# A layer kernel: the long convolution's result written over its padded input, two more PSUM banks for the last fill products, and a diagonal product in two fp32r parts

## The chip, the cores and the metric

The kernel runs on one core of one Trainium2 chip. The metric is the device time of one execution in microseconds (us), and the time of a kernel is the median of its runs. A core has five engines with an instruction stream each: PE (TensorE, matrix products; its weight loads are shown apart as PEld), DVE (VectorE), ACT (ScalarE), POOL (GpSimd) and SP (SyncE, which here issues the DMAs). Each engine works through its own instructions in a fixed order and waits where the next one needs a result or a buffer that is not there yet. Products are summed in PSUM, which has eight banks of 128 partitions by 512 fp32 numbers.

## The reference, cut to what matters

One layer over 1024 tokens of width 1024. A modulated norm feeds one input projection, and its columns feed three mixers: a neighbourhood attention, a short gated convolution and a Conformer branch with a 31-tap depthwise convolution and a layer norm behind it. The three are merged by gates, and an output projection follows.

```python
def dw_conv(x, w):
    k = w.shape[0]
    return lax.conv_general_dilated(x, w[:, None, :].astype(x.dtype), window_strides=(1,),
        padding=[((k - 1) // 2, k // 2)], dimension_numbers=('NWC', 'WIO', 'NWC'),
        feature_group_count=x.shape[-1])

def conformer_branch(z, w_conv, b_conv, ln_g, ln_b):
    a, g = z[..., C_GLU:C_GLU + D_BRANCH], z[..., C_GLU + D_BRANCH:C_Z]
    u = dw_conv(a * jax.nn.sigmoid(g), w_conv) + b_conv
    u = jax.nn.silu(layer_norm(u, ln_g, ln_b))
    return u * jax.nn.silu(z[..., C_Z:GATES])

def merge_branches(z, ya, yb, yc, w_out_a, w_out_b, w_out_c, w_o):
    ga, gb, gc = jnp.split(jax.nn.sigmoid(z[..., GATES:]), N_BRANCH, axis=-1)
    m = ga * (ya @ w_out_a) + gb * (yb @ w_out_b) + gc * (yc @ w_out_c)
    return m @ w_o

# hybrid_layer
h, gate = modulate(x, c, lp['norm_g'], lp['w_ada'], lp['b_ada'])
z = h @ lp['w_in']
x = x + gate * merge_branches(z, ya, yb, yc, lp['w_out_a'], lp['w_out_b'], lp['w_out_c'], lp['w_o'])
```

## The kernel before

**Numbers in two parts.** Nearly every product of two fp32 matrices is done as three products of type fp32r: both factors are split into a rounded part (`wh`, `bh`: an ACT copy) and the rest (`wl`, `bl`: a subtraction on DVE or POOL), and wh·bh, wh·bl and wl·bh are summed in one bank. `split` does this. So each weight tile costs ACT a copy and DVE or POOL a subtraction before PE can use it. One product of 128 rows by 512 columns over a depth of 512 is 12 matmuls in a row.

**The stages.** Up to about 490 us the norm, the q, k and v projections and the attention run. Beside the attention PE is kept filled with "fill" products: `first_quarters` computes, for 20 of the 22 pairs of column tiles that come later, the product of one quarter (24 matmuls in two parts of 12, `quarter_part`) into a bank `qps` and sends each part's result to memory (`p1d` after part 0, `c11d` or `gd` after part 1). The last `BEHIND` = 4 fill products stand after the attention (L817). From 513 us on `group` (L885 to L945) is run 22 times, with seven multiplications of halves in place of eight, some of them already done by the fill: PE computes the products `gf`, `gc`, `gd`, `ge`, DVE adds them up (`u2` L919, `v` L923, and `c22`, `c12`, `c21` in `add`, L876), and a second product is summed into the bank of `gd` once `c22` has been read from it. PE's order puts the products `ge`, `gf` and `gc` between the end of `gd` and that second product (`gd<-hb`). Behind the groups come the merges of the three branches (`merge(1)`, `merge(0)`, `merge(2)`, with the products `ops` of L108 to L110) and the output projection, to the end.

**The parts the change touches.** `quarter_bank` (L684) gives each fill product a PSUM bank: every third one the single bank of `ps_q`, the others the two of `ps_m`. The attention's own banks are free once it is over. `conv_steps` (L834) is the 31-tap convolution: four channel tiles, each with a padded input `upad` (128x1056, two buffers, loaded by a DMA from `ud`), an accumulator `cv` in two PSUM banks that all four tiles share, and 31 DVE instructions (tap 0 at L844, the others at L846). `group` takes three steps of it at each of two places and two more in whole groups. Behind the last tap ACT adds the bias and writes the two halves of the result into tiles `cvo` (L850), a DMA each takes them to memory (L851), and only then may tap 0 of the next tile write `cv`. The `cvo` tiles have the tag "ev": four buffers, shared with `u2`, `v` and others. `norm_steps` (L1259) is the layer norm behind the convolution, done in small steps beside the merges. It needs one number per token in every partition: DVE writes 1/std on the diagonal of four 128x128 blocks (`diag`, L1285), and PE multiplies by a matrix of ones (L1291, in plain fp32).

**What sets the order.** The program is written in the order above, but a scheduler orders every engine's instructions by its own estimate of when each could run. An edit at one place can therefore move instructions elsewhere. Within one engine the resulting order is fixed before the run.

Of the kernel before, what the change touches and what calls it, by code (L numbers as in the profile page):

```python
# [8 lines left out]
F32 = mybir.dt.float32  # L9
F32R = mybir.dt.float32r  # L10
BF16 = mybir.dt.bfloat16
AF = mybir.ActivationFunctionType
ALU = mybir.AluOpType
AX = mybir.AxisListType
PSUM = bass.MemoryType.PSUM
DRAM = bass.MemoryType.DRAM

P = 128
# [28 lines left out]
def tile_hybrid(ctx: ExitStack, tc, x, xT, cx, cond, crow, ng, w_ada, b_ada, wqkv, wz,  # L47
                wout, wo, qg, kg, rpbs, mask, cs, cf, cfb, lng, lnb, out):
    nc = tc.nc
    pe, act, dve, pool = nc.tensor, nc.scalar, nc.vector, nc.gpsimd  # L50
# [9 lines left out]
    mctx = ExitStack()  # L60
# [10 lines left out]
    def const(src, shape, name):  # L71
        t = cst.tile(shape, F32, name=name)
        nc.sync.dma_start(t, src)
        return t


    def rsqrt_mean(dst, ss, n, k):

        pool.tensor_scalar(out=dst, in0=ss, scalar1=1.0 / n, scalar2=EPS, op0=ALU.mult, op1=ALU.add)  # L79
        state["pow"] = pool.tensor_tensor(out=dst, in0=dst, in1=half_neg[:, :k], op=ALU.pow)  # L80
# [41 lines left out]
    cvd = [dram.tile([P, S], F32, name=f"cvd{i}") for i in range(4)]  # L122
# [3 lines left out]
    B512 = [slice(0, 512), slice(512, 1024)]  # L126
# [26 lines left out]
    state = {"wp": wp}  # L153
# [108 lines left out]
    def hcols(part, k, sl):  # L262

        o = sl.start // 512
        return hlf[o][k][:, part, sl.start - o * 512 : sl.stop - o * 512]
# [265 lines left out]
    with tc.tile_pool(name="at", bufs=1, reuse_waits="tile") as at, \  # L531
# [151 lines left out]

        def quarter_bank():  # L684
            state["qb"] = state.get("qb", 0) + 1
            if state["qb"] % 3 == 0:
                return ps_q.tile([P, 512], F32, tag="q", name="qps")
            return ps_m.tile([P, 512], F32, tag="m", name="qps")
# [21 lines left out]
        def first_quarters(ns):  # L710

            begun = None
            for n in (*ns, None):
                new = None
                if n is not None:
                    new = n, load_w(wz[lead(n)], KT, pool), quarter_bank()
                    quarter_part(0, *new)
                if begun:
                    quarter_part(1, *begun)
                begun = new  # L720
# [33 lines left out]
        for step, (n0, n1) in enumerate(zip(cuts, cuts[1:])):  # L754
# [3 lines left out]
            elif step == 2:  # L758
                for j in range(4):
                    hi, lo = hcols(0, j, B512[1]), hcols(1, j, B512[1])  # L760
# [10 lines left out]
    cfb_t = const(cfb, [P, 4], "cfb_t")  # L771
# [3 lines left out]
    def s512(name, tag="s", bufs=5, dt=F32):  # L775
        return sp.tile([P, 512], dt, tag=tag, name=name, bufs=bufs)

    def split(hi, lo, src, eng):
        act.copy(hi, src)  # L779
        eng.tensor_tensor(out=lo, in0=src, in1=hi.bitcast(F32), op=ALU.subtract)  # L780
# [32 lines left out]
    for src in (early[0], early_s[1]):  # L813
        ahead.append([s512(n, "hs", 4, F32R) for n in ("ah", "al")])
        split(*ahead[-1], src, dve)
    with tc.issue_after(state["py"].ins):
        first_quarters(ahead_of[-BEHIND:])  # L817
    mctx.close()
# [15 lines left out]
    def conv_steps():  # L834
        for i in range(4):
            u = sp.tile([P, 1056], F32, tag="upad", name="upad", bufs=2)
            pool.memset(u[:, 0:15], 0.0)
            pool.memset(u[:, 1039:1056], 0.0)
            nc.sync.dma_start(u[:, 15:1039], ud[i])
            acc = ps_c.tile([P, S], F32, tag="cv", name="cv")  # L840
            for j in range(31):
                src = u[:, j : j + S]
                if j == 0:
                    dve.tensor_scalar(out=acc, in0=src, scalar1=cf_t[:, i, 0:1], scalar2=None, op0=ALU.mult)  # L844
                else:
                    dve.scalar_tensor_tensor(out=acc, in0=src, scalar=cf_t[:, i, j : j + 1], in1=acc, op0=ALU.mult, op1=ALU.add)  # L846
                yield
            for b in range(2):
                y = ev("cvo")
                act.activation(y, acc[:, B512[b]], AF.Identity, bias=cfb_t[:, i : i + 1])  # L850
                nc.sync.dma_start(cvd[i][:, B512[b]], y)  # L851

    conv = conv_steps()

    def conv_step(n):
# [23 lines left out]
    def ev(name):  # L879
        return sp.tile([P, 512], F32, tag="ev", name=name, bufs=4)  # L880
# [208 lines left out]
    def b_start(n, i):  # L1089
        u = sp.tile([P, 1026], F32, tag="bu", name="bu", bufs=1)  # L1090
        pool.memset(u[:, 0:1], 0.0)
        pool.memset(u[:, 1025:1026], 0.0)
        held = {}

        def meet(b, t):
            if b == 0 and b not in held and n not in c11d:
                c = tmp("c11")
                act.copy(c, t)
                t = c
            if b in held:  # L1100
                pool.tensor_tensor(out=u[:, 1 + b * 512 : 513 + b * 512], in0=held[b], in1=t, op=ALU.mult)
            held[b] = t

        run(CG + i, BV + i, meet, meet, n=ahead_n(n))
        return u
# [19 lines left out]
    for n, (kind, i, j) in enumerate(plan):  # L1125
        kw = {"n": ahead_n(n)}
        if kind == "b_start":
            u = b_start(n, i)
# [18 lines left out]
    bp = ctx.enter_context(tc.tile_pool(name="bp", bufs=1, reuse_waits="tile"))  # L1147
# [8 lines left out]
    ones = bp.tile([P, P], F32, name="ones")  # L1156
    onesr = bp.tile([P, P], F32R, name="onesr")
# [3 lines left out]
    def loaded(src, name, t=None):  # L1161
        t = big(name) if t is None else t
        nc.sync.dma_start(t, src)
        return t
# [65 lines left out]
    def ltmp(name):  # L1230
        return bp.tile([P, 512], F32, tag="ltmp", name=name, bufs=2)

    def col_sums(src_fn, res):
        for b in range(2):
            ps = ps_l.tile([P, 512], F32, tag="l", name="sums")
            ready = []

            def total(i, hi, lo):
                pe.matmul(ps, onesr, hi, start=i == 0, stop=False)
                pe.matmul(ps, onesr, lo, start=False, stop=i == 3)  # L1240

            for i in range(4):
                s = src_fn(i, b)
                hi = bp.tile([P, 512], F32R, tag="lnh", name="lnh", bufs=3)
                lo = bp.tile([P, 512], F32R, tag="lnl", name="lnl", bufs=3)
                split(hi, lo, s, dve)
                ready.append((i, hi, lo))
                if i:
                    total(*ready.pop(0))
                yield  # L1250
            total(*ready.pop(0))
            res.append(ps)
# [6 lines left out]
    def norm_steps():  # L1259
        sums = []  # L1260
        yield from col_sums(lambda i, b: cv[i][:, B512[b]], sums)
        for b in range(2):
            for i in range(4):
                dve.scalar_tensor_tensor(out=cv[i][:, B512[b]], in0=sums[b], scalar=-1.0 / 512, in1=cv[i][:, B512[b]], op0=ALU.mult, op1=ALU.add)
                yield
        sums = []
        yield from col_sums(square, sums)
        var = small[:, :KT]
        for b in range(2):
            for t in range(4):  # L1270
                j = ltmp("junk")
                dve.tensor_tensor_reduce(j[:, :P], sums[b][:, t * P : (t + 1) * P], ident, 1.0, 0.0, ALU.mult, ALU.add,
                                         var[:, b * 4 + t : b * 4 + t + 1])
            yield
        yield
        yield
        rsqrt_mean(var, var, 512, KT)
        for _ in range(3):
            yield
        rstd = []  # L1280
        diags = []
        for b in range(2):
            j = ltmp("diag")
            for t in range(4):
                dve.tensor_scalar(out=j[:, t * P : t * P + P], in0=ident, scalar1=var[:, b * 4 + t : b * 4 + t + 1], scalar2=None, op0=ALU.mult)  # L1285
            diags.append(j)
        for _ in range(4):
            yield
        for b in range(2):
            ps = ps_l.tile([P, 512], F32, tag="l", name="rstd")  # L1290
            pe.matmul(ps, ones, diags[b], start=True, stop=True)  # L1291
            rstd.append(ps)
        yield
        for i in range(4):
            z = loaded(zcd[i], "zcin")
            yh, yl_ = (of("yb", n) for n in ("ych", "ycl"))
            for b in range(2):
                c = cv[i][:, B512[b]]
                dve.tensor_tensor(out=c, in0=rstd[b], in1=c, op=ALU.mult)
                act.activation(c, c, AF.Silu, bias=lnb_t[:, i : i + 1], scale=lng_t[:, i : i + 1])  # L1300
                yield
                pool.tensor_tensor(out=z[:, B512[b]], in0=z[:, B512[b]], in1=c, op=ALU.mult)
                split(yh[:, B512[b]], yl_[:, B512[b]], z[:, B512[b]], dve)
                yield
            yc_s.append((yh, yl_))

    def gate_steps():
# [11 lines left out]
        dve.tensor_scalar(out=gate, in0=gate, scalar1=0.5, scalar2=None, op0=ALU.mult)  # L1319

    steps = norm_steps()
    gsteps = gate_steps()

# [211 lines left out]
```

## Time and profile before

| what | value |
|---|---|
| runs | 1091.55, 1084.32, 1086.27 us |
| median | 1086.27 us |
| the profiled execution's own time | 1085.42 us |
| its span, first to last instruction | 1083.6 us |
| mean granted TensorE clock | 0.997 |
| ACT busy | 563.7 us, 52% of the span |
| POOL busy | 636.7 us, 59% of the span |

All durations below come from that one profiled execution, whose own time is 0.85 us under the median. A row of the timeline gives the start, the length, the engine, the line, the operation, its output and inputs (out<-in), and in brackets the idle time before it with what ended it. SPq is SP's queue of DMA issues. A row of the windows gives a stretch, its length, and each engine's busy time in it with the number of its instructions in brackets, then the granted clock (1.00 is full speed), the share of the DMA engines' time and GB/s.

### The profile page before, as it was taken

The numbers are of one execution on the slowest core, as the hardware profiler recorded it, in microseconds if no ns is written. First come the engines' busy times: TensorE is split into PE (matmuls) and PEld (weight loads), VectorE is DVE, ScalarE is ACT, GpSimd is POOL, SyncE is SP. The second block draws the span as 40 slices with busy tenths as digits, with TensorE's granted clock in tenths as the row PEclk, the third lists the DMA queues.
The fourth block names the chain that finished last, engine by engine and source line by source line (L and its number), as shares of the span: only waits on it lengthen the run. The fifth ranks groups of instructions, "written<-read, shape, count | busy, mean of one in ns | idle before, by whom it ended". The sixth has DMA issues, their size and how long they took to land.

```text
span 1083.6 us, 16063 instructions
## 1 busy us (share of the span) xinstructions
PE 1062.7 (98%) x5280; PEld 909.8 (84%) x5280; DVE 769.5 (71%) x1260; ACT 563.7 (52%) x1195; POOL 636.7 (59%) x662
## 2 busy tenths in 40 slices
PE   7999999999999999999999999999999999999998
PEld 5888998998999888887888888887888888888886
DVE  6985577766665655534994998997973469988664
ACT  6865666666656676656443334233345534425730
POOL 3155966536626497433898787985685461623670
PEclk9999999999999999999999999999999999999999
DMA  9838413313313356449646446465555988461362
GB/s 351 287 138 283 152 49 122 104 53 101 104 63 93 108 175 199 155 139 323 231 146 197 153 143 223 170 196 183 167 173 165 331 344 296 137 246 66 98 226 104
DMA packets 93859, 189.40 MB, mean 175 GB/s; under 512 B 11888, under 2 KB 36848, under 8 KB 93680
## 3 DMA queue, kind: packets, MB, share of 16 engines
q1 hardware_dynamic: 89168, 186.28, 50.9%
q10 hardware_dynamic: 4608, 2.10, 0.7%
q8 instruction: 42, 0.69, 0.3%
q14 instruction: 41, 0.34, 0.1%
HBM read 140.10 MB, written 50.79 MB: 176 GB/s over the span
## 4 chain that ended last, share of the span: by engine, by line
PE 82%; DMA 2%; ACT 1%; DVE 1%; SPq 1%; POOL 0%; issue 0%; ACTq 0%; POOLq 0%; DVEq 0%
PE ops L109 4%; PE ops L108 4%; PE ops L110 4%; PE gd L870 4%; PE gd L871 4%; PE gd L872 4%; PE qps L694 3%; PE py L651 3%; PE qps L695 3%; PE qps L696 3%; PE pp L631 3%; PE ps L108 2%; PE ps L110 2%; PE ps L109 2%; PE ge L871 2%; PE gf L871 2%
## 5 line engine op out<-in xcount | busy, mean ns | idle before, releaser
L846 DVE SCALAR_TENSOR_TENSOR cv<-upad,cf_t,cv 128x1024 f32<-128x1024 f32 x120 | 153.6, 1280 | 1.0
L91 POOL TENSOR_TENSOR wl<-wr,wh 128x384 fp32r<-128x384 f32 (+1 forms) x87 | 85.7, 995 | 68.6 <-ACT wh L89 53.9
L780 POOL TENSOR_TENSOR wl<-s,wh 128x512 fp32r<-128x512 f32 x83 | 109.3, 1328 | 18.4 <-ACT wh L779 14.4
L779 ACT CAST wh<-s 128x512 fp32r<-128x512 f32 x111 | 66.1, 610 | 95.5 <-POOL s L783 39.6
L634 DVE TENSOR_TENSOR plo<-pp,phi 128x256 fp32r<-128x256 f32 (+2 forms) x96 | 54.5, 575 | 43.8 <-ACT phi L633 43.1
L694 PE MATMUL qps<-ha,wh 128*128 128x512 f32 x160 | 63.2, 396 | 1.4 <-ACT quarter L701 1.3
L89 ACT CAST wh<-wr 128x384 fp32r<-128x384 f32 (+1 forms) x96 | 45.6, 484 | 36.0 <-PE qps L695 14.3
L695 PE MATMUL qps<-ha,wh 128*128 128x512 f32 x160 | 63.4, 396 | 0.0
L696 PE MATMUL qps<-ha,wl 128*128 128x512 f32 x160 | 63.0, 396 | 0.0
L590 POOL TENSOR_TENSOR bias<-mk,img 64x96 f32<-64x96 bf16 (+1 forms) x96 | 45.3, 478 | 27.8 <-DVE mn L616 23.7
L633 ACT CAST phi<-pp 128x256 fp32r<-128x256 f32 (+2 forms) x96 | 46.7, 495 | 16.6 <-PE pp L631 16.1
L617 ACT ACTIVATE pt<-sc,mn 128x256 f32<-128x256 f32 x64 | 30.4, 475 | 35.7 <-DVE mn L616 33.1
L631 PE MATMUL pp<-ident,pt 128*128 128x128 f32 x304 | 48.0, 272 | 0.4 <-DVE plo L634 0.2
L79 POOL TENSOR_SCALAR ssh<-ssh 128x4 f32<-128x4 f32 (+1 forms) x40 | 13.2, 331 | 59.7 <-DVE ssh L254 57.7
L780 POOL TENSOR_TENSOR wl<-wro,wh 128x512 fp32r<-128x512 f32 x12 | 16.7, 1390 | 53.7 <-ACT wh L779 46.9
L616 DVE CUSTOM_DVE_ANT_0 pt<-sl,bias,mn 128x384 f32<-128x384 f32 (+1 forms) x64 | 37.2, 581 | 13.5 <-PE sl L613 12.4
L631 PEld LDWEIGHTS pp<-ident,pt 128*128 128x128 f32 x304 | 38.2, 140 | 8.8 <-DVE plo L634 1.0
L624 DVE TENSOR_SCALAR pt<-pt,mn 128x640 f32<-128x640 f32 (+1 forms) x64 | 43.6, 722 | 1.0
L80 POOL TENSOR_TENSOR ssh<-ssh,half_neg 128x4 f32<-128x4 f32 (+1 forms) x40 | 39.8, 996 | 3.0
L870 PE MATMUL gd<-hb,wh 128*128 128x512 f32 x96 | 37.4, 390 | 2.1 <-DVE c L876 2.1
L108 PE MATMUL ps<-wh,hb 128*128 128x384 f32 x112 | 38.5, 344 | 0.5 <-ACT rawc L223 0.5
L110 PE MATMUL ps<-wh,hb 128*128 128x384 f32 x112 | 38.1, 345 | 0.5 <-DVE hb L384 0.5
(441 smaller groups left out, 3753.1 us busy)
## 6 DMA issues: line engine op xcount, KB each, us to landing
wr<-in_wz SPq DMA_DIRECT2D x34, 512.0 KB, 3.8
gs<-gd SPq DMA_DIRECT2D x24, 512.0 KB, 5.0
wada<-in_w_ada SPq DMA_DIRECT2D x22, 512.0 KB, 8.6
wr<-in_wz SPq DMA_DIRECT2D x52, 192.0 KB, 2.6
wrf<-in_wo SPq DMA_DIRECT2D x16, 512.0 KB, 3.5
cht<-chd SPq DMA_DIRECT2D x24, 256.0 KB, 3.0
wro<-in_wout SPq DMA_DIRECT2D x24, 256.0 KB, 4.5
p1d<-quarter SPq DMA_DIRECT2D x20, 256.0 KB, 2.8
```

Source lines behind the costliest of these rows:

```text
L91: lo_eng.tensor_tensor(out=lo[:, :n], in0=raw[:, :n], in1=hi[:, :n].bitcast(F32), op=ALU.subtract)
L108: pe.matmul(ps, ah, bh, start=i == 0, stop=False)
L110: pe.matmul(ps, al, bh, start=False, stop=i == n - 1)
L631: pe.transpose(out=pp[:, c * P : c * P + P], in_=src, identity=ident)
L694: pe.matmul(ps, wh, bh, start=k == 0, stop=False, skip_group_check=True)
L695: pe.matmul(ps, wh, bl, start=False, stop=False, skip_group_check=True)
L696: pe.matmul(ps, wl, bh, start=False, stop=k % 4 == 3, skip_group_check=True)
L779: act.copy(hi, src)
L780: eng.tensor_tensor(out=lo, in0=src, in1=hi.bitcast(F32), op=ALU.subtract)
L846: dve.scalar_tensor_tensor(out=acc, in0=src, scalar=cf_t[:, i, j : j + 1], in1=acc, op0=ALU.mult, op1=ALU.add)
L870: pe.matmul(ps, wh, bh, start=first and j == 0, stop=False, skip_group_check=True)
L871: pe.matmul(ps, wh, bl, start=False, stop=False, skip_group_check=True)
```

## The change

It has three parts. The fill products of odd count take a bank of a new pool of two banks, once that pool is open; it is opened behind the attention, so it serves the last four. The convolution's result goes into the first 1024 columns of the padded input instead of two `cvo` tiles, and the ACT instructions and DMAs are issued in the same step as the last tap, not in the next one. The diagonal of the norm is split like other factors (one ACT copy, one DVE subtraction for each half) and multiplied by `onesr`, the fp32r matrix of ones, in two products that are summed.

```diff
         def quarter_bank():
             state["qb"] = state.get("qb", 0) + 1
+            if "ps_e" in state and state["qb"] % 2:
+                return state["ps_e"].tile([P, 512], F32, tag="e", name="qps", bufs=2)
             if state["qb"] % 3 == 0:
                 return ps_q.tile([P, 512], F32, tag="q", name="qps")
             return ps_m.tile([P, 512], F32, tag="m", name="qps")
...
+    state["ps_e"] = mctx.enter_context(tc.tile_pool(name="ps_e", bufs=1, space=PSUM))
     with tc.issue_after(state["py"].ins):
         first_quarters(ahead_of[-BEHIND:])
...
-                yield
+                if j < 30:
+                    yield
             for b in range(2):
-                y = ev("cvo")
-                act.activation(y, acc[:, B512[b]], AF.Identity, bias=cfb_t[:, i : i + 1])
-                nc.sync.dma_start(cvd[i][:, B512[b]], y)
+                act.activation(u[:, B512[b]], acc[:, B512[b]], AF.Identity, bias=cfb_t[:, i : i + 1])
+                nc.sync.dma_start(cvd[i][:, B512[b]], u[:, B512[b]])
+            yield
...
-            diags.append(j)
+            hi = bp.tile([P, 512], F32R, tag="lnh", name="dgh", bufs=3)
+            lo = bp.tile([P, 512], F32R, tag="lnl", name="dgl", bufs=3)
+            split(hi, lo, j, dve)
+            diags.append((hi, lo))
...
         for b in range(2):
             ps = ps_l.tile([P, 512], F32, tag="l", name="rstd")
-            pe.matmul(ps, ones, diags[b], start=True, stop=True)
+            for i, part in enumerate(diags[b]):
+                pe.matmul(ps, onesr, part, start=i == 0, stop=i == 1)
             rstd.append(ps)
```

The changed kernel's lines lie a few numbers on: L701 becomes L703, L704 L706, L707 L709, L779 L781, L780 L782, L783 L785, L844 L847, L846 L849, L850 L853, L876 L880, L919 L923, L935 L939, L1078 L1082, L1291 L1299. The numbers behind a name (`qps_6210`) only tell tiles apart. "x2" behind a row stands for two instructions alike.

The order of ACT's instructions at the last fill products, before. `T3` are factors of the groups to come that a DMA brings and ACT copies, `wry` the first group's weights, which a DMA brings, `ah` and `s4` are made from them or from `wry`'s sums, and `quarter` is a fill product's result. `qps_6210` is the last fill product's bank:

```order
L779 CAST T3_6002<-T3_6002 128x512
L779 CAST T3_6003<-T3_6003 128x512
L779 CAST ah_6048<-wry_6040 128x512
L935 COPY s4_6375<-wry_6040 128x512
L701 COPY quarter_6223<-qps_6210 128x512
L707 COPY quarter_6239<-qps_6160 128x512
L779 CAST ah_6052<-s2_6045 128x512
```

The same place after (the last fill product's bank is `qps_6213`):

```order
L781 CAST T3_6001<-T3_6001 128x512
L709 COPY quarter_6141<-qps_6077 128x512
L703 COPY quarter_6176<-qps_6163 128x512
L781 CAST T3_6002<-T3_6002 128x512
L781 CAST T3_6003<-T3_6003 128x512
L706 ACTIVATE quarter_6192<-qps_6112 128x512
L781 CAST ah_6048<-wry_6040 128x512
L939 COPY s4_6379<-wry_6040 128x512
L703 COPY quarter_6226<-qps_6213 128x512
L709 COPY quarter_6242<-qps_6163 128x512
L781 CAST ah_6052<-s2_6045 128x512
```

The copy of the last product's part 0 (`quarter_6226`) still stands behind `ah` and `s4`. On PE, which is not shown, all four part 0 products now come first and then the four part 1 products, where before the last product's part 0 came after two part 1 products. On SP the issue of one fill result (`p1d18`, 256 KB) moves from ahead of the twelve loads of the T factors and the two of `wry` to just behind them.

ACT where the convolution's first tile ends, before (`cv_6350` is its accumulator):

```order
L779 CAST wh_7121<-s3_7049 128x512
L779 CAST wh_7148<-s4_7144 128x512
L850 ACTIVATE cvo_6974<-cv_6350,cfb_t_5987 128x512
L935 COPY s4_7275<-wr_7173 128x512
L779 CAST wh_7188<-s2_7178 128x512
L850 ACTIVATE cvo_6977<-cv_6350,cfb_t_5987 128x512
```

And after (`cv_6354`):

```order
L781 CAST wh_6957<-wrs_6791 128x512
L781 CAST wh_6990<-s3_6918 128x512
L853 ACTIVATE upad_6350<-cv_6354,cfb_t_5987 128x512 x2
L781 CAST wh_7017<-s4_7013 128x512
L939 COPY s4_7146<-wr_7043 128x512
L781 CAST wh_7060<-s2_7048 128x512
```

The two instructions now stand together, one group earlier. DVE at the start of the second tile, before:

```order
L919 TENSOR_TENSOR u2_6932<-gf_6915,p1_6904 128x512
L923 TENSOR_TENSOR v_6951<-gc_6934,u2_6932 128x512
L780 TENSOR_TENSOR wl_7149<-s4_7144,wh_7148 128x512
L783 TENSOR_TENSOR s4_7275<-s4_7275,s2_7178 128x512
L876 TENSOR_TENSOR c21_6969<-gd_6859,u2_6813 128x512
L844 TENSOR_SCALAR cv_6984<-upad_6980,cf_t_5985 128x1024
L846 SCALAR_TENSOR_TENSOR cv_6984<-upad_6980,cf_t_5985,cv_6984 128x1024
```

And after, where the last rows of the first tile stand close ahead of it:

```order
L880 TENSOR_TENSOR c22_6750<-gd_6733,v_6706 128x512
L849 SCALAR_TENSOR_TENSOR cv_6354<-upad_6350,cf_t_5985,cv_6354 128x1024
L880 TENSOR_TENSOR c12_6777<-ge_6760,v_6706 128x512
L849 SCALAR_TENSOR_TENSOR cv_6354<-upad_6350,cf_t_5985,cv_6354 128x1024
L923 TENSOR_TENSOR u2_6817<-gf_6800,p1_6787 128x512
L847 TENSOR_SCALAR cv_6986<-upad_6982,cf_t_5985 128x1024
L927 TENSOR_TENSOR v_6836<-gc_6819,u2_6817 128x512
```

The second tile's tap 0 now comes one instruction behind the first tile's last tap. The third and fourth tiles' tap 0 move the same way, each some two groups earlier than before.

PE at the norm's diagonal product, before (`ops` is a merge product):

```order
L110 MATMUL ops<-ya,wl 128x512
L1291 MATMUL rstd<-diag,ones 128x512
L108 MATMUL ops<-ya,wh 128x512
L109 MATMUL ops<-ya,wh 128x512
L1291 MATMUL rstd<-diag,ones 128x512
```

And after:

```order
L110 MATMUL ops<-ya,wl 128x512
L1299 MATMUL rstd<-dgh,onesr 128x512
L108 MATMUL ops<-ya,wh 128x512
L109 MATMUL ops<-ya,wh 128x512
L110 MATMUL ops<-ya,wl 128x512
L108 MATMUL ops<-ya,wh 128x512
L1299 MATMUL rstd<-dgh,onesr 128x512
L1299 MATMUL rstd<-dgl,onesr 128x512
```

The product with the second `dgl` follows eight merge matmuls later.

## The prediction, made before the changed kernel was run

> **What bounds the kernel now.** I read the page's head and its chain first, then PE's waits, then stretches of time where PE is not full, and last the timeline at those places.
>
> ```profile
> PE 1062.7 (98%) x5280; PEld 909.8 (84%) x5280; DVE 769.5 (71%) x1260; ACT 563.7 (52%) x1195; POOL 636.7 (59%) x662
> PE 82%; DMA 2%; ACT 1%; DVE 1%; SPq 1%; POOL 0%; issue 0%; ACTq 0%; POOLq 0%; DVEq 0%
> ...
> PE xT_ps L371 <- DVE xt L363: 4.5, 4, 2.0
> PE gd L870 <- DVE c L876: 2.1, 1, 2.1
> PE qps L694 <- ACT quarter L701: 1.3, 1, 1.3
> ```
>
> PE is busy for 1062.7 of 1083.6 us, so only two things can shorten the kernel: one of the 20.9 us in which PE idles, or fewer or shorter matmuls. The waits (total, times, longest) name two idle places that the change could touch, 2.1 us at `gd` and 1.3 us at `qps`. The largest, `xT_ps`, is in the kernel's beginning and is left alone. The windows say the same:
>
> ```profile
> 500.00:520.00 20.00, 18.59 (x82) 14.73 (x81) 14.23 (x18) 13.02 (x24) 7.64 (x6) 1.00 0.99 361
> 740.00:760.00 20.00, 17.92 (x80) 14.56 (x79) 15.84 (x18) 7.29 (x13) 10.78 (x9) 1.00 0.56 182
> 920.00:940.00 20.00, 20.00 (x86) 15.84 (x85) 17.55 (x40) 9.24 (x16) 10.84 (x9) 1.00 0.41 133
> ```
>
> The first number behind the comma is PE's busy time: 1.41 us are missing at the last fill products, 2.08 at the convolution, none at the norm's diagonal. So the change has at most 3.5 us of idle time to win, and at the diagonal only what its matmuls become shorter. The other engines are off the path while their lateness is covered.
>
> **Part 1, the two banks.**
>
> ```profile
> 510.56 0.50 PE L694 MATMUL qps<-ha,wh 128*128 128x512 f32 x1 [1.29 <-ACT quarter L701]
> ...
> 508.88 0.62 ACT L779 CAST ah<-wry 128x512 fp32r<-128x512 f32 x1 [1.31 <-DMA wry<-in_wz]
> 509.41 0.58 ACT L935 COPY s<-wry 128x512 f32<-128x512 f32 x1
> 509.93 0.58 ACT L701 COPY quarter<-qps 128x512 f32<-128x512 f32 x1
> ...
> 491.62 0.38 SPq L708 DMA_DIRECT2D gd<-quarter  x1
> 493.24 0.32 SPq L708 DMA_DIRECT2D p1d<-quarter  x1
> 493.61 7.71 SPq L799 DMA_DIRECT2D T<-td  x12
> 501.68 1.02 SPq L807 DMA_DIRECT2D wry<-in_wz  x2
> ...
> 492.00:494.00 2.00, 2.00 (x11) 1.65 (x10) 0.00 (x0) 0.81 (x2) 1.27 (x7) 1.00 1.03 396
> ```
>
> Part 1 of the last fill product waits for the copy of its part 0 (L701), which ends at 510.51. A missing bank is not all of it: ACT has stood idle for 1.31 us behind the `ah` cast, which waits for the DMA of `wry`, and the copy stands two instructions behind that. The new order keeps `ah` and `s4` ahead of that copy, although its product is done several us sooner. So the end of PE's wait is still set by when `wry` lands. What makes `wry` earlier is SP's queue: one 256 KB store moves from ahead of the loads to behind them. The DMA engines are full there (share 1.03, 396 GB/s), so 256 KB less ahead of `wry` is 262144 B / 396 GB/s = 0.66 us. The T loads also need not wait for that store's copy, but with the engines full an earlier issue moves nothing more. Bounds: 0, if the store's place turns out not to matter, and 1.4, the whole missing time. I take **0.7 us**, nearest to the DMA row. The bytes per second hang on no page; the Trainium skill ("DMA: Bandwidth & Descriptors", section "Where 436 GB/s comes from") puts the memory side's limit for a core at about 358 GB/s, which the row above, 396, does not bear out; by it the term would be an estimated 0.73 us.
>
> The same edit moves the convolution's tap 0 ahead of the `al` that product `gf` needs:
>
> ```profile
> 513.51 1.11 DVE L780 TENSOR_TENSOR al<-s,ah 128x512 fp32r<-128x512 f32 x1
> 514.54 1.27 DVE L844 TENSOR_SCALAR cv<-upad,cf_t 128x1024 f32<-128x1024 f32 x1
> 516.14 0.39 PE L870 MATMUL gf<-T,ah 128*128 128x512 f32 x1
> ```
>
> `al` is done at 514.62 and first read by `gf`'s third matmul, two pitches of 0.23 us after 516.14, at 516.6: 2.0 us to spare, and tap 0 costs 1.27. With PE 0.7 us earlier nothing is left over, but `wry`, from which `al` comes, is earlier by the same amount. I cost it at 0. If that cover fails, it costs the shortfall, some tenths.
>
> **Part 2, the convolution.**
>
> ```profile
> 742.78 0.69 ACT L850 ACTIVATE cvo<-cv,cfb_t 128x512 f32<-128x512 f32 x1 [6.10 <-DMA cvd<-cvo]
> 743.50 1.29 DVE L844 TENSOR_SCALAR cv<-upad,cf_t 128x1024 f32<-128x1024 f32 x1 [5.99 <-ACT cvo L850]
> 746.02 0.68 DVE L876 TENSOR_TENSOR c<-gd,v 128x512 f32<-128x512 f32 x1
> ...
> 736.46 0.39 PE L870 MATMUL ge<-hb,wh 128*128 128x512 f32 x1
> 744.39 0.39 PE L872 MATMUL gc<-T,wl 128*128 128x512 f32 x1
> 746.85 0.47 PE L870 MATMUL gd<-hb,wh 128*128 128x512 f32 x1 [2.08 <-DVE c L876]
> ...
> cvd<-cvo SPq DMA_DIRECT2D x2, 256.0 KB, 3.3
> ...
> ACT cvo L850 <- DMA cvd<-cvo: 15.7, 4, 6.1
> DVE cv L844 <- ACT cvo L850: 12.7, 3, 6.0
> ```
>
> These rows are one chain. ACT could not write the second `cvo` since no "ev" buffer was free until a DMA had landed (6.10 us of waiting). Tap 0 of the last tile waited for ACT (5.99), and behind tap 0 in DVE's order stood tap 1 and `c22`, which empties `gd`'s bank for PE's next product. PE had `ge`, `gf` and `gc` to do meanwhile, 736.46 to 744.62, so DVE could be 8.2 us late for nothing, and the 2.08 us are what went beyond. From matmul to matmul 744.39 to 746.85 is 2.46, less one pitch of 0.23: 2.2 us lost.
>
> Now ACT writes into `upad`, which is at hand, in the step of the last tap; the 15.7 us of waits on landed stores lose their cause. The eight ACT instructions (0.69 each) and eight stores stay, only sooner. What is new: a padded buffer comes free when its stores have landed, not with its last tap. POOL's two small memsets and SP's next load of `upad` wait for that, and weight loads stand behind the load on SP. From its issue a store takes 3.3 us to land (the row on `cvd`). The buffer is not needed until a whole other tile (31 taps) is done, and the weights behind have a cover that let ACT's and DVE's 6 us waits pass here with only 2.2 reaching PE. I cost this at 0; without cover it would cost 3.3 for each of the two buffers that are used again, 6.6 in all.
>
> The pause between two tiles goes as well, and with it DVE's time to catch up:
>
> ```profile
> 574.00:597.00 23.00, 23.00 (x103) 19.06 (x102) 7.88 (x13) 7.37 (x13) 19.29 (x18) 1.00 0.61 211
> ...
> 597.00:617.00 20.00, 20.00 (x89) 16.54 (x89) 19.49 (x20) 7.63 (x13) 15.66 (x13) 1.00 0.41 128
> 617.00:637.00 20.00, 20.00 (x90) 16.57 (x89) 18.39 (x22) 7.21 (x13) 13.84 (x11) 1.00 0.64 216
> 637.00:661.00 24.00, 24.00 (x108) 19.87 (x107) 22.63 (x26) 10.17 (x17) 20.30 (x16) 1.00 0.29 99
> ```
>
> Between the first tile's end and the second's start DVE (the third busy time) worked 7.88 of 23 us; in the second tile 60.5 of 64. With the pause filled DVE has some 5% to spare instead of falling idle, and PE is full in all these rows. So I take the whole **2.2 us**; bounds 0 (the wait comes back elsewhere) and 2.2.
>
> **Part 3, the diagonal.**
>
> ```profile
> 929.40 0.39 PE L110 MATMUL ops<-ya,wl 128*128 128x512 f32 x1
> 929.63 1.02 PE L1291 MATMUL rstd<-diag,ones 128*128 128x512 f32 x2
> 932.05 0.40 PE L108 MATMUL ops<-ya,wh 128*128 128x512 f32 x1
> 932.28 0.39 PE L109 MATMUL ops<-ya,wh 128*128 128x512 f32 x1
> ...
> 925.52 0.62 ACT L779 CAST wh<-wro 128x512 fp32r<-128x512 f32 x1 [5.50 <-PE ops L109]
> 928.47 0.70 DVE L1191 SCALAR_TENSOR_TENSOR ops<-gs,ops 128x512 f32<-128x512 f32 x1 [0.57 <-PE ops L110]
> ```
>
> Starts of like matmuls are 0.23 us apart (932.05, 932.28), though each is shown as 0.39 long, so I count pitches. From 929.40 to 932.05 are 2.65 us, in which stand four `ops` matmuls (0.92) and two plain fp32 products, shown as two records each: 1.73, or 0.87 a product. Four fp32r products in their place are 4 x 0.23 = 0.92. PE is full here, so **0.8 us** come off its path. The Trainium skill ("FP8 and Floating Point Precision", section "TensorE Precision Notes") says that true fp32 takes four passes through the array; by it a product would be 0.92 and the gain an estimated 0.92 us. The trace, with 0.87, nearly agrees.
>
> Added are two ACT casts (0.62 each), with ACT idle for 5.50 us there, and two DVE subtractions (0.70 each). DVE stands idle 0.57 us just before 928.47 and so can be about that late at no cost, and the second `dgl` product stands eight matmuls later on PE. Bounds: 0, if PE waits for a `dgl`, and 0.92. I take 0.8.
>
> **The sum.** 0.7 + 2.2 + 0.8 = 3.7 us from 1085.42 gives 1081.7. That execution lies 0.85 under the median of the three runs, so the prediction in their terms is 1082.6 us. A measurement of this kernel tells about 1%, 11 us, from no change; all three gains together are a third of that.
>
> **The rivals.**
>
> 1. *The copy of the fill result is not on the DMA's clock at all* (the store's place does not matter, or `al` gives back the gain). For it: `ah` stays ahead of the copy. Against it: full DMA engines. Then 2.2 + 0.8 come off: 1083.3. Chance 0.2.
> 2. *The whole fill wait goes*, since the earlier loads bring `wry` forward by 1.4 us: T loads could be issued from 492.0, behind the store of 491.62, 1.6 us sooner. Against it: full engines. 1.4 + 2.2 + 0.8 = 4.4: 1081.9. Chance 0.12.
> 3. *The convolution's stall only moves*, so that the change doesn't do what it says: tap 0 still waits, now for two ACT copies (1.4 us) that stand behind casts which wait for POOL, at another place. For it: DVE up to 95% busy. Then 0.7 + 0.8: 1084.8. Chance 0.12.
> 4. *Slower: DVE falls behind.* Place: the groups of the second and third tile, where no pause is left. Each us of `c22` beyond the 8.2 us of cover is a us of PE. Had DVE to do 60.5 us of work in less than the 64 that PE gives it, lateness would add up from tile to tile. It outweighs the 3.7 once lateness reaches 11.9 us, and at 14 costs 5.8: 1088.4. Against it: DVE stayed under 95% and PE full at that density. Chance 0.06.
>
> **How the numbers follow.** The forecast, all three parts as sized, has a chance of 0.5, and rivals 1 to 4 have 0.5 together. From the lowest of the runs, 1084.32, the best sum of 4.5 gives 1079.8, and I put the low end at 1079.5. The upper end takes in rival 3 at 1084.8 and the scatter of medians that runs from 1084.3 to 1091.6 allow: 1087.5. Outside lie rival 4 and a median of high runs, together under 0.2. Faster by over 1% means under 1075.4, beyond every sum here: 0.02. Slower by over 1% means above 1097.1, which rival 4 reaches only with lateness over 23 us or waits for landed stores in several tiles: 0.02. The rest, 0.96, is within 1%.
>
> **What would show it.** In the new profile the 740 to 760 window should have PE at 20.00, and the waits no `cvo` on a landed store. The wait at `qps` should be about 0.7, with `ah` still waiting for `wry`. At the diagonal four records with a pitch of 0.23. The prediction is wrong if `gd` waits for `c` longer than 2.1 in all, if PE waits for a `wh` or `wl` between 570 and 800, or if `gf` waits for `al` at 515.

## The result, and the profile after

| | median | lowest to highest | runs |
|---|---|---|---|
| before | 1085.62 us | 1080.81 to 1091.55 | 21 |
| after | 1081.00 us | 1079.53 to 1084.00 | 21 |

The ratio of after to before is 0.9964, with a 95% interval of 0.9953 to 0.9975: 3.9 us less, between 2.7 and 5.1. (The two medians lie 4.6 us apart; the ratio on record, here and below, is not the quotient of the two medians.) The prediction was 1082.6 us and 3.7 us less. The profiled execution of after took 1082.91 us, 1.9 over its median, with a span of 1081.1 us.

The windows of the kernel after, at the three places that the prediction showed of before (stretch, length, then PE, PEld, DVE, ACT and POOL busy, the granted clock, DMA share, GB/s):

```profile
500.00:520.00 20.00, 19.52 (x86) 15.72 (x85) 14.66 (x19) 13.64 (x25) 9.04 (x7) 1.00 1.03 386
740.00:760.00 20.00, 20.00 (x90) 16.58 (x89) 19.86 (x22) 8.67 (x15) 15.46 (x13) 1.00 0.54 176
920.00:940.00 20.00, 20.00 (x90) 16.58 (x89) 18.29 (x40) 11.04 (x18) 11.01 (x9) 1.00 0.40 135
```

At the convolution PE is full, at the diagonal 90 matmuls stand in 20 us where 86 stood, and at the fill 0.48 us are missing instead of 1.41. These are the three places of the change. How much of the first row belongs to one execution alone is told below.

To put a size to each part I count from landmark to landmark on PE: S, the start of the attention's last matmul (`py` times `vc`); F from there to the first `ga` matmul (the fill); G from there to ACT's first copy of `px` (the groups with the convolution); H from there to PE's last matmul (the merges with the diagonal, the output).

| profile | S | F | G | H |
|---|---|---|---|---|
| before | 489.20 | 24.22 | 315.39 | 250.62 |
| after | 491.09 | 23.07 | 313.07 | 249.77 |
| after less before | +1.89 | -1.15 | -2.32 | -0.85 |

S holds work that the change does not touch, and it differs by some us from execution to execution (487.94 to 496.22 over all profiles here), so it is left aside. The rest adds up to 4.3 us. The prediction had 0.7, 2.2 and 0.8. But these are two executions, and a row of before that looked like a property of the kernel was not one, as the runs below show.

At the fill the kernel after still waits in this profile, and for the same copy, with `ah` ahead of it:

```profile
511.30 0.50 PE L696 MATMUL qps<-ha,wh 128*128 128x512 f32 x1 [0.47 <-ACT quarter L703]
...
509.63 0.62 ACT L781 CAST ah<-wry 128x512 fp32r<-128x512 f32 x1 [0.32 <-DMA wry<-in_wz]
510.15 0.58 ACT L939 COPY s<-wry 128x512 f32<-128x512 f32 x1
510.68 0.58 ACT L703 COPY quarter<-qps 128x512 f32<-128x512 f32 x1
...
493.94 7.58 SPq L801 DMA_DIRECT2D T<-td  x12
502.79 1.00 SPq L809 DMA_DIRECT2D wry<-in_wz  x2
```

Counted from S, the T loads are issued at 2.85 us instead of 4.41, `ah` starts at 18.54 instead of 19.68.

At the end of the first tile of the convolution, in the same profile:

```profile
573.18 1.28 DVE L849 SCALAR_TENSOR_TENSOR cv<-upad,cf_t,cv 128x1024 f32<-128x1024 f32 x1
...
574.58 1.26 ACT L853 ACTIVATE upad<-cv,cfb_t 128x512 f32<-128x512 f32 x2
575.87 1.29 DVE L847 TENSOR_SCALAR cv<-upad,cf_t 128x1024 f32<-128x1024 f32 x1 [0.82 <-ACT upad L853]
575.49 0.86 SPq L854 DMA_DIRECT2D cvd<-upad  x2
580.93 0.32 SPq L842 DMA_DIRECT2D upad<-ud  x1
581.01 0.11 POOL L840 MEMSET upad<- 128x15 f32 x1 [0.78 <-DMA cvd<-upad]
```

And its waits (total, times, longest) of ACT at the result:

```profile
ACT upad L853 <- DVE cv L849: 4.3, 3, 3.0
```

The last tap (L849) ended at 574.46, and 1.4 us later tap 0 of the next tile runs, where it was 596.84 before. ACT waits for the last tap only, and for no store. The new wait that the prediction named is there too: the memset of the padded input, and SP's load behind it, now wait for the stores to land at about 581, 5 us after their issue, where the prediction had reckoned with 3.3. SP stands at most 2.7 us for it and POOL 0.78, and PE does not feel it: it is busy for 340.0 of the 340 us from 520 to 860.

At the diagonal the matmuls follow each other at one pitch:

```profile
928.51 0.39 PE L110 MATMUL ops<-ya,wl 128*128 128x512 f32 x1
928.73 0.39 PE L1299 MATMUL rstd<-dgh,onesr 128*128 128x512 f32 x1
928.96 0.39 PE L108 MATMUL ops<-ya,wh 128*128 128x512 f32 x1
```

### The profile page after: what moved, and what is told of

The parts are those of the page before. It is cut to its first block, busy times and chain, and to the rows that moved or that the text cites. A ratio compares the mean times of both kernels' runs of the same rounds, so it can differ in the third digit from the quotient of the medians.

```text
span 1081.1 us, 16068 instructions
## 1 busy us (share of the span) xinstructions
PE 1062.2 (98%) x5280; PEld 910.0 (84%) x5280; DVE 771.0 (71%) x1262; ACT 567.9 (53%) x1197; POOL 633.4 (59%) x662
## 4 chain that ended last, share of the span: by engine, by line
PE 85%; DMA 5%; DVE 4%; ACT 3%; issue 1%; SPq 1%; POOL 1%; ACTq 0%; POOLq 0%; DVEq 0%
PE gd L876 4%; PE ops L109 4%; PE ops L108 4%; PE gd L875 4%; PE gd L874 4%; PE ops L110 4%; PE py L651 3%; PE qps L696 3%; PE pp L631 3%; PE qps L697 3%; PE ps L110 3%; PE qps L698 3%; PE ps L108 3%; PE ps L109 3%; PE gf L876 2%; PE gc L876 2%
## 5 line engine op out<-in xcount | busy, mean ns | idle before, releaser
L849 DVE SCALAR_TENSOR_TENSOR cv<-upad,cf_t,cv 128x1024 f32<-128x1024 f32 x120 | 153.9, 1282 | 0.9
L782 POOL TENSOR_TENSOR wl<-s,wh 128x512 fp32r<-128x512 f32 x83 | 108.7, 1319 | 18.4 <-ACT wh L781 18.1
L781 ACT CAST wh<-s 128x512 fp32r<-128x512 f32 x111 | 67.1, 611 | 96.9 <-PE gc L875 24.7
L634 DVE TENSOR_TENSOR plo<-pp,phi 128x256 fp32r<-128x256 f32 (+2 forms) x96 | 54.6, 575 | 44.2 <-ACT phi L633 43.5
L782 POOL TENSOR_TENSOR wl<-wro,wh 128x512 fp32r<-128x512 f32 x12 | 16.6, 1385 | 60.3 <-ACT wh L781 55.2
L109 PE MATMUL ps<-wl,hb 128*128 128x384 f32 x112 | 38.2, 341 | 0.0
```

What stands on the lines that cost most here:

```text
L109: pe.matmul(ps, ah, bl, start=False, stop=False)
```

## The experiments

For each kernel F, G and H come from its one profiled execution, "time" from runs beside the kernel before on the same chip, with the 95% interval of the ratio.

**The two banks alone.** Of the diff only the first two hunks.

```diff
+            if "ps_e" in state and state["qb"] % 2:
+                return state["ps_e"].tile([P, 512], F32, tag="e", name="qps", bufs=2)
...
+    state["ps_e"] = mctx.enter_context(tc.tile_pool(name="ps_e", bufs=1, space=PSUM))
```

> Only the two banks. Stretches are counted on PE from start to start: F from the attention's last matmul (py, plo times vc) to the first ga matmul, 24.22 us before and 23.07 after the whole change; G from there to ACT's first copy of px, 315.39 and 313.07; H from there to PE's last matmul, 250.62 and 249.77. Theory 1 (the banks alone bring the whole of F, through the earlier loads of T and wry): F 23.1, G 315.4, H 250.6, the time 1.1 lower. Theory 2 (part of F's gain is an accident of one execution, or comes of the convolution's edit): F 23.5 to 24.2, the time 0 to 0.7 lower.

Measured: F 22.50, G 315.15, H 250.62; time 1082.26 against 1084.36 us, 0.9978 (0.9962 to 0.9994). G and H are untouched, as both theories had it. F is lower than the whole change's 23.07, which neither had: the fill differs from execution to execution. The ratio makes the time 2.4 us lower (0.7 to 4.1), more than the 0.4 by which F is lower in the mean of the profiles compared below; where the rest comes from stays open.

**Only the place of the result.** The result goes into the padded input, in the same step as before.

```diff
-                y = ev("cvo")
+                y = u[:, B512[b]]
```

> Only the place of the convolution's result: it is written into the padded input, but still in the step behind the last tap. Theory 1 (the buffer is what counts): the two ACT instructions move ahead as in the whole change, G 313.1, no wait of ACT on a landed store, the time 2.3 lower, F 24.2, H 250.6. Theory 2 (the earlier step is what counts): G 315.4, the time as before.

Measured: F 22.94, G 313.07, H 251.82; time 1081.40 against 1084.36 us, 0.9968 (0.9953 to 0.9983). G is that of the whole change to the hundredth: theory 1. (H is 1.2 us too long in this execution. Some 0.6 of that is a wait of the norm's sums at 880 to 900 us, which single profiles of other kernels show as well.)

**Only the step.** The result goes to `cvo` as before, but in the step of the last tap.

```diff
-                yield
+                if j < 30:
+                    yield
             for b in range(2):
                 y = ev("cvo")
                 act.activation(y, acc[:, B512[b]], AF.Identity, bias=cfb_t[:, i : i + 1])
                 nc.sync.dma_start(cvd[i][:, B512[b]], y)
+            yield
```

> Only the step: the result still goes into cvo tiles, but ACT's instructions and the stores are written down in the same step as the last tap. Theory 1 (the buffer counts): the wait on the landed store stays, PE waits about 2.1 us at gd, G 315.4, the time as before. Theory 2 (the step counts): G 313.1, the time 2.3 lower.

Measured: F 22.37, G 314.60, H 250.61; time 1084.16 against 1084.36 us, 0.9993 (0.9978 to 1.0008). Its waits (total, times, longest):

```profile
ACT cvo L851 <- DMA cvd<-cvo: 14.9, 4, 6.2
DVE cv L844 <- ACT cvo L851: 13.1, 3, 6.1
...
PE gd L872 <- DVE c L878: 1.2, 1, 1.2
```

The chain of before is all there. Behind the first tile's last tap, which ends at 572.1, ACT's two instructions still start only at 588.87 and 594.46, behind other work. That the scheduler puts them there because it reckons with the buffer's wait is likely, but not shown. So the buffer counts and the step does not. That PE waits 1.2 us here and 2.1 in the first profile is the next hint that single waits vary.

**The diagonal alone.** The last two hunks of the diff.

> Only the diagonal in two fp32r products for each half. Theory 1 (each matmul on PE's path is paid by its pitch): H 249.8, the time 0.8 lower, F 24.2, G 315.4. Theory 2 (the two DVE subtractions push back something that PE needs later): H between 249.8 and 251.5, the time -0.8 to +0.9.

Measured: F 22.54, G 315.54, H 249.80; time 1083.20 against 1084.36 us, 0.9980 (0.9966 to 0.9995). H is 0.82 lower: theory 1. The two ACT casts and two DVE subtractions cost nothing that H shows. (The ratio says 2.2 us, between 0.5 and 3.7; the 0.8 lies inside.)

**One buffer of its own.** The kernel before, with a buffer for the result that nothing else uses.

```diff
-                y = ev("cvo")
+                y = sp.tile([P, 512], F32, tag="cvo", name="cvo", bufs=1)
```

> The kernel before, but the convolution's result goes through one buffer of its own instead of the four that it shares with u2, v and others. Theory 1 (the shared ring made ACT wait): ACT waits only for the first half's own store, about 3.3 us a tile, tap 0 starts earlier, PE's wait at gd is gone, G 313.1 to 313.6, the time 1.8 to 2.3 lower. Theory 2 (any wait of tap 0 on a landed store is too late for PE): PE still waits at gd, G 314 to 316.

Measured: F 22.55, G 313.07, H 250.59; time 1080.93 against 1085.02 us, 0.9967 (0.9953 to 0.9980).

```profile
DVE cv L844 <- ACT cvo L850: 9.7, 3, 4.2
ACT cvo L850 <- DMA cvd<-cvo: 9.2, 3, 3.5
```

No wait of PE at `gd` is left, and G is again 313.07. ACT still waits 3.5 us for the landing of the first half's store and tap 0 up to 4.2 for ACT, and that is covered. So what cost PE was not a wait on a store as such, but that the four shared buffers made it 6 us at a time when DVE was already late: in the group ahead of the last tile `u2` started 4.58 us behind the end of `gf` in the first profile of before, and 0.09 here. Writing in place does the same without the buffer.

**More work for DVE.** The whole change, with one line of each group run four times.

```diff
-        dve.tensor_tensor(out=u2, in0=f, in1=p1, op=ALU.add)
+        for _ in range(4):
+            dve.tensor_tensor(out=u2, in0=f, in1=p1, op=ALU.add)
```

> The whole change, with u2 computed four times over in each group instead of once (three more DVE instructions of 0.60 us a group, 22 groups, 39.6 us of DVE work). DVE has 272 us of work in the 340 us from 520 to 860 before this. Theory 1 (DVE is far from being the bound, its lateness counts only beyond 8.2 us, and the taps give way): G 313.1 to 315, the time up by less than 2. Theory 2 (DVE without pauses is at its limit while the convolution runs): 229 us of work in 240 becomes some 260, lateness grows by 20 us, of which 12 reach PE: the time up by 12.

Measured: F 22.24, G 315.29, H 249.80; time 1083.91 against 1085.02 us, 0.9994 (0.9980 to 1.0008). The longest of PE's waits from 500 us on (total, times, longest):

```profile
PE gf L874 <- DVE u L924: 1.2, 1, 1.2
```

And two windows, with DVE's busy time the third:

```profile
740.00:760.00 20.00, 20.00 (x90) 16.57 (x89) 19.17 (x24) 8.35 (x15) 13.89 (x12) 1.00 0.60 193
760.00:860.00 100.00, 100.00 (x443) 82.81 (x442) 71.10 (x93) 45.78 (x79) 58.76 (x46) 1.00 0.57 197
```

39.6 us of DVE work cost PE 2.2 us of G, a little over theory 1 and far from the 12 of theory 2. The taps give way: the last one ends at 808.9, where the change alone has 767.0, so the convolution runs on into DVE's idle time behind it (71.1 us busy in 760 to 860, where the change alone has 42.8).

**One store more ahead of the loads.** The whole change, and behind the store of the last attention tile:

```diff
             nc.sync.dma_start(yad[hp], ya.rearrange("p r c -> p (r c)"))
+            if hp == 3:
+                spare = dram.tile([P, 512], F32, name="spare")
+                nc.sync.dma_start(spare, ya.rearrange("p r c -> p (r c)")[:, :512])
```

> The whole change, and one store more of 256 KB (half of the last attention tile, into memory that nobody reads), issued just ahead of the T loads, with nothing new to wait for. Theory 1 (bytes count: what the two banks won was the store moved from ahead of the loads to behind them): wry lands 0.66 us later, F 23.7, the time 0.6 over the whole change. Theory 2 (the issue time counts: the loads had stood on SP behind a store that waited for its copy, 1.6 us): F 23.1 to 23.3, the time as with the whole change.

Measured: F 22.21, G 313.08, H 250.53; time 1081.53 against 1085.02 us, 0.9971 (0.9958 to 0.9984). Neither theory: with 256 KB more ahead of `wry`, PE does not wait at the fill at all. But the run does not price the bytes, because the edit also moved ACT's order. The copy of the last product's part 0, for which PE waits elsewhere, now stands ahead of `ah`:

```profile
506.86 0.59 ACT L706 COPY quarter<-qps 128x512 f32<-128x512 f32 x1
507.32 0.64 ACT L784 CAST ah<-wry 128x512 fp32r<-128x512 f32 x1
507.84 0.61 ACT L942 COPY s<-wry 128x512 f32<-128x512 f32 x1
```

So PE no longer depends on `wry` there. `wry` itself landed 17.99 us behind S, which lies among the landings of the profiles with the two banks (17.02 to 18.51, below).

**The third set of T factors behind the fill.** The whole change, and:

```diff
-    for i in (1, 0, 2):
+    for i in (1, 0):
         load_t(T[i], i)
...
         first_quarters(ahead_of[-BEHIND:])
+    load_t(T[2], 2)
```

> The whole change, and the third set of T factors is loaded behind the fill products, so that wry's two loads stand four 256 KB loads sooner in SP's queue and ACT's copies of the fill results no longer stand behind T casts of that set. Theory 1 (PE's last wait at the fill is set by when wry lands): the 0.63 us that are left of it go, F 22.4, the time 0.6 under the whole change, if gd's T factors still land in time. Theory 2 (the wait has another cause): F 23.1. If T comes too late: G grows by what PE then waits at gd of the first group, up to 1 us.

Measured: F 22.23, G 313.07, H 249.80; time 1080.56 against 1085.02 us, 0.9966 (0.9952 to 0.9980). PE has no wait left at the fill, and none at `gd` for the later factors. F fits theory 1: `wry` lands at 14.46 us behind S, some 3 us sooner. But a repeat of the whole change, below, has the same F without this edit.

**How much the fill differs.** Four profiles more, two of before, one of after and one of the kernel above:

> The kernel before, once more, to see how far the fill's wait differs between executions. The sum of PE's losses between the attention's last matmul and the first ga was 1.95 us in its first profile, and 0.1 to 0.7 in the three kernels of the single parts that leave the fill as it was. Theory 1 (1.95 was one execution in which wry landed late): 0.1 to 0.8 here, F 22.3 to 23.0. Theory 2 (the other edits took the wait away): 1.7 to 2.0, F 24.

> The kernel before in one execution more. Theory 1: losses of 0.1 to 0.8 us at the fill, F 22.3 to 23.0. Theory 2: 1.7 to 2.0, F 24.

> The whole change once more, on the chip of r4. Theory 1 (wry's landing differs between executions): losses at the fill between 0 and 0.8 us, F 22.2 to 23.0; G 313.1, H 249.8. Theory 2 (the first profile's 0.74 is what the banks leave): F 23.0 to 23.1.

> The change with the third set of T factors loaded behind the fill, beside r3_after on the same chip. If its fill never waits: F 22.2 again, and the time 0 to 0.8 under r3_after, by what r3_after loses at the fill. If its freedom from waits was luck: F up to 23.

Measured: the first repeat of before F 22.82, G 314.71, H 250.61, its time 1082.60 us; the second F 22.67, G 316.95, H 252.51, its time 1087.18; after F 22.21, G 313.08, H 250.44, time 1080.14 against 1084.52 us, 0.9966 (0.9949 to 0.9982); the T loads behind the fill F 22.25, G 313.07, H 249.77, time 1080.83, 0.9970 (0.9954 to 0.9987). The last was expected to be up to 0.8 us faster than after and is 0.7 slower, within the noise; with both F at 22.2 there was nothing to win.

All F side by side, by the fill's order, each with the time behind S at which the first of `wry`'s two loads landed:

| | fill as before | fill with the two banks |
|---|---|---|
| F | before 24.22, its repeats 22.82, 22.67 | after 23.07, its repeat 22.21 |
| `wry` landed | 19.61; 18.21, 18.07 | 18.51; 17.02 |
| F | place 22.94, step 22.37, diagonal 22.54, own buffer 22.55 | banks alone 22.50, DVE load 22.24 |
| `wry` landed | 18.32, 17.76, 17.91, 17.93 | 17.93, 17.26 |
| means | F 22.87, landed 18.26 | F 22.51, landed 17.68 |

(The extra store, 22.21, and the T loads behind the fill, 22.23 and 22.25, have another order of loads or copies and stand outside.) In the fill as before, F is the landing plus 4.60 to 4.63 us in all seven profiles: PE's restart is set by `wry` every time. With the two banks that holds where `wry` lands late (23.07 and 22.50, the landing plus 4.56 and 4.57). Where it lands at 17.26 or sooner PE does not wait, and F stands at 22.2, its length without a wait.

The first profile of before is the odd one. Its `ah` waited 1.31 us for `wry` and started 19.68 us behind S; in the "step" kernel, with the same order of the fill, it started at 17.84, 0.08 behind the landing, after 0.12 us of idle time that the row does not name:

```profile
507.72 0.63 ACT L779 CAST ah<-wry 128x512 fp32r<-128x512 f32 x1
508.25 0.58 ACT L937 COPY s<-wry 128x512 f32<-128x512 f32 x1
508.77 0.58 ACT L701 COPY quarter<-qps 128x512 f32<-128x512 f32 x1
```

The windows from 500 to 520 say why: the DMA engines were about as full, but moved less. First the "step" kernel, then the first repeat of before:

```profile
500.00:520.00 20.00, 20.00 (x90) 16.34 (x89) 15.27 (x19) 13.70 (x25) 8.59 (x8) 1.00 1.03 397
```

```profile
500.00:520.00 20.00, 19.69 (x88) 15.97 (x87) 15.90 (x20) 12.62 (x24) 9.05 (x8) 1.00 1.03 392
```

The last number of each row is GB/s: 397 and 392 at a share of 1.03, where the first profile of before moved 361 at 0.99. Theory 1 of the repeats holds. What made the DMAs slower in that one execution is not seen in its profile and stays open.

## Why the prediction was right, and where it was not

**The convolution, 2.2 us predicted.** Right in size, and in mechanism but for the step. G is 313.07 or 313.08 in all seven profiles of kernels whose result has a place of its own and DVE its usual work, and 314.60 to 316.95 in the six that keep the shared buffers. The mean of those, 315.4, makes the gain 2.3; without the highest, in which the granted clock fell (last section), the mean is 315.1 and the gain 2.0. The step, which the prediction took together with the place ("in the step of the last tap"), contributes nothing. The stores behind the memsets and SP's load, costed at 0 for lack of need, take 5 us to land and cost PE nothing.

**The diagonal, 0.8 us predicted.** Right: 0.82 and 0.85, and H is 249.77 to 249.80 in five of the seven profiles with it. In the other two, the repeat of after (250.44) and the extra store (250.53), PE waits 0.31 and 0.41 us for the norm's sums at about 894, ahead of the diagonal. Profiles without the diagonal's edit show that wait too (0.55 in the run of the place alone, 0.65 and 0.55 in the second repeat of before), so it is not counted to it. What covers the added ACT and DVE instructions was named and holds.

**The fill, 0.7 us predicted.** The wait was right, its size was not. "So the end of PE's wait is still set by when `wry` lands" holds in every profile with the fill as before. What failed is the size of the idle time behind it: the prediction took the 1.41 us that one execution missed for a property of the kernel. In the other six with that order F is 22.65 in the mean, only 0.44 over its length without a wait (22.21), so 0.66 us could not come off it in the mean. The first profile's 24.22 stands 1.6 over that mean, because `wry` landed 1.6 later than in the mean of the six (19.61 against 18.03), a slow spell of the DMAs. With the two banks `wry` lands 0.58 us sooner in the mean (0.35 without the first profile of before), near the 0.66 of the 256 KB, but the single landings scatter by 1.9 and 1.5 us, so this does not show the price. F is lower by 22.87 less 22.51, 0.4 us, or by 0.14 without the first profile of before. Seven and four values that reach over 1.9 and 0.9 us do not part either from zero, nor the store's place from the loads that are issued 1.6 us sooner. That 0.7 comes near 0.4 is luck.

**The sum.** 0.4 + 2.3 + 0.8 = 3.5 us, inside the interval of 2.7 to 5.1. The predicted 3.7 lies in it as well. The times of the single parts cannot size them: by their ratios the banks, the place and the diagonal alone bring 2.4, 3.5 and 2.2 us, some 8 together and twice the whole change, each with an interval some 3 us wide.

**The rivals.** Rival 1, no gain at the fill, is not ruled out in its number, but its reason is: PE's restart does hang on the DMA of `wry`. Rival 2, the whole fill wait gone, came true in the repeat of after, and its reason, the 1.4 us by which earlier loads bring `wry` forward, did not in the mean: T is issued 1.56 us sooner and `wry` lands 0.35 to 0.58 sooner. Rival 3, a stall that only moves, is out: no `gd` wait is left in any profile of the new order. Rival 4, DVE falling behind without pauses, is turned round. Rows of before and after at the group where `u2` is latest behind the end of `gf`:

```profile
741.67 0.39 PE L872 MATMUL gf<-T,wl 128*128 128x512 f32 x1
750.92 0.68 DVE L919 TENSOR_TENSOR u<-gf,p 128x512 f32<-128x512 f32 x1
```

```profile
658.09 0.39 PE L876 MATMUL gf<-T,wl 128*128 128x512 f32 x1
662.62 0.68 DVE L923 TENSOR_TENSOR u<-gf,p 128x512 f32<-128x512 f32 x1
```

Before, `u2` started 8.9 us behind the end of `gf` (750.92 less 742.06), after at most 4.1 (662.62 less 658.48). The pauses between tiles were not time to catch up. In the three of them (574 to 597, 660 to 670, 733 to 743.5) DVE was busy for 17.0 of 43.5 us, while the taps that it could have done were left for later. The tiles' ends came later, and from the second tile's start to the last tile's end `u2` was 4.0 to 8.9 us behind the end of `gf`, after 0.8 to 4.1.

## What to carry to other kernels

A gain that is read from one idle stretch should be sized only after asking whether that stretch is in every execution: the one that ended with a DMA while all DMA engines were full cost PE 0.2 to 2.0 us here, by the execution, while the one that ended with DVE's fixed order came back in all six profiles of that order (1.2 to 2.2 us). Where a result waits for a shared ring of buffers, a dead buffer that is at hand (here its own input) takes the wait away, and here it did not matter in which step the code says so. An engine that pauses and is then late, like DVE here, is helped by starting sooner, and its load over the whole stage said more than its load in the busy part.

## What the runs showed of the hardware that was not expected

A stall of PE can cost more than itself. In the second repeat of before PE waited at `gd` as always, and then the granted clock fell:

```profile
744.00:746.00 2.00, 0.85 (x4) 0.75 (x5) 2.00 (x3) 0.96 (x2) 0.14 (x1) 1.00 0.01 2
746.00:748.00 2.00, 2.00 (x8) 1.55 (x7) 2.00 (x3) 1.32 (x3) 1.29 (x1) 0.62 0.72 217
748.00:750.00 2.00, 2.00 (x6) 1.61 (x5) 1.97 (x3) 1.10 (x2) 1.29 (x1) 0.53 0.87 287
750.00:752.00 2.00, 2.00 (x10) 1.63 (x9) 2.00 (x3) 0.00 (x0) 0.22 (x1) 1.00 0.96 331
```

The wait was 1.97 us, the clock 0.62 and 0.53 in the 4 us behind it, with 14 matmuls there instead of 22, and G was 3.9 us over the 313.07 that it has without a wait, where the other five profiles with the shared buffers were 1.5 to 2.5 over it. In those five (1.2 to 2.2 us of wait) the clock stayed at 1.00. The Trainium skill ("TensorE: Matmul & The Clock Gate", section "Part 1: The HAM clock gate (the "warmup" mystery)") says that the gate follows how busy PE has been lately, by a window that runs freely. A fall in one execution of six at a like wait fits that. The idle window that this section of the Trainium skill gives for a throttled clock, some 3.4 us, is longer than the wait of 1.97 us, so here the measurement differs from it. The removed stall is worth about 2.0 us in five of the six executions and 3.9 in the one.

In the last profile of the T loads behind the fill, a DVE instruction of the attention (`pt`, in the stretch of 8.57 us below) took 8.1 us once, where its like take 0.55, and PE stood 4.4 us for it. The granted clock was 0.50 from 414 to 420, behind that wait. The timeline:

```profile
406.62 8.57 DVE L624 TENSOR_SCALAR pt<-pt,mn 128x640 f32<-128x640 f32 x2
414.88 0.88 PE L631 MATMUL pp<-ident,pt 128*128 128x128 f32 x3 [4.42 <-DVE pt L624]
```

That execution took 1087.30 us, the longest of those profiled. Such things, which no edit here touches, are why the parts were sized from stretches and not from single times.
